# Scan products on whole fp32 operands, a raw weight ring of four, and scan and convolution work dealt out in a fixed order

## The chip, the core and the metric

The kernel runs on one core of one Trainium2 chip. Time is device time in microseconds of one execution, as the median over runs; the kernel before took 1641.52 us (three runs, 1640.8 to 1644.02). The profile is of one further execution of the same program. Engines are named as in the profile: PE (TensorE matmul), PEld (its weight loads), DVE (VectorE), ACT (ScalarE), POOL (GpSimd), SP (the engine whose queue issues most DMAs).

## The reference

One encoder block over 1040 tokens (16 learned meta tokens ahead of 1024 frames) of width 1024, all in float32:

```python
h = h + token_mixer(rmsnorm(h, norm_mix_g), ...)
h = h + channel_mixer(rmsnorm(h, norm_ffn_g), ...)
return rmsnorm(h, norm_final_g)[:, N_META:]
```

The token mixer projects the stream to queries, keys, values and gates of eight heads. Four heads are an mLSTM (queries and keys go through a causal convolution over four tokens and silu; learned input and forget gates with a running maximum), four are a retention with rotary positions and a fixed decay per head. Both are evaluated in chunks, with a state that goes from chunk to chunk:

```python
# mLSTM, one chunk: q, k (C, 128), v (C, 256), state c_st (128, 256), n_st (128)
s = (q @ k.T) * w_intra
num = s @ v + w_inter[:, None] * (q @ c_st)
den = s.sum(-1) + w_inter * (q @ n_st)
h = num / maximum(abs(den), exp(-m_row))[:, None]
c_st = decay * c_st + (w_src[:, None] * k).T @ v
n_st = decay * n_st + (w_src[:, None] * k).sum(0)
# retention: the same without den, with fixed decays in place of the gates
```

Each head's output is normalised per token, multiplied by a gate (sigmoid or silu), and all heads are projected back to width 1024 by w_out. The channel mixer is a gated MLP of width 2816 with a causal convolution over three tokens.

## The kernel before

**Products.** A float32 product is made of three fp32r matmuls: an operand x is split into hi, its rounding to fp32r, by ACT, and lo = x - hi by DVE, and `mm3` and `mm3s` (L487 to L501) sum hi*hi, hi*lo and lo*hi in one PSUM bank. Large projections are cut in the manner of Strassen and Winograd into seven block products (`ROWS`, L545), with sums of the weight blocks made on DVE (`u_fm`, L252) or by accumulating DMAs on POOL's queue (`insum`, L315; `wsum`, L304).

**Stages.** After the first norm and the projection of head 4, the token mixer goes through the heads in the order 4, 0, 1, 2, 3, 5, 6, 7 (`HEADS`; 0 to 3 are mLSTM, 4 to 7 retention), of which (0, 1), (2, 3) and (5, 6) are pairs. For each pair there are a group of query and key steps of the first head (`qk_steps`, 14 steps of 12 matmuls), a group of value steps for both (`v_steps`, 28 steps), the gate steps of the first head (`o_steps`, 14), and the query and key steps and gate steps of the second. Head 7 has a group of its own for values. Then the output product with w_out runs (`mixw`, a `Seven`, L841; its loop at L1475), in steps "1", "65", "73", "4", "2", and the MLP behind it.

**Scan.** A head has nine chunks (16 meta tokens, then eight of 128 tokens; `CH`). `scan_a` (L1052) makes a chunk's scores s = k q and the transposed key, scales and splits them (pt, kw, qd; `split` at L1044). `scan_b` (L1087) splits the values into the ring `vring` (`v_split`, L654), computes the state's update u and the output n by `mm3`, evicts n, forms the new state C and splits it (S). `post_steps` (L1128) normalise a head's chunks, transpose them and multiply by the gate (`sigt`); for all heads but 7 the result goes to DRAM (`mxd`).

**Order.** The tile framework places each engine's instructions by their order in the program and a timeline that it computes; an ordering dependency without a semaphore pins two instructions to each other (`after`, L81). `merge` (L1188) puts the scan steps of one head (`tasks`, L1271; each step is `scan_a` of the next chunk and `scan_b` of this one) between the product steps of the next groups. `gates` (L735), `qk_final` (convolution or rotary, L712) and `tables_make` (L698) each come as one block between groups. Head 7's post steps come behind all product steps (L1416), and the loads for the output product and of the residual behind them (L1419 to L1456).

**Weights.** Units (a weight's load and split) stand in a list and are issued when `need` (L214) asks for one of them, with those whose sizes add up to five places ahead. Raw tiles of 512 KB come from a pool with two slots (`raw_tile`, L181), split tiles from one with three. Among the units are the meta tokens' value products on raw fp32 weights (`meta_raw`, L347: vm), the last two tokens' part of the output product (`last_two`, L288: m; ACT scales a w_out row into two split tiles, which POOL's queue accumulates in DRAM as accd), and the first operands of the output product (`first_right`, L330: r). Loads go through SP's queue in their order.

```python
71    wraw = ctx.enter_context(tc.tile_pool(name="wraw", bufs=2))
225   while i + 1 < len(units) - len(fu) and place[units[i + 1][0]][1] <= j + 5:
226       i += 1
```

Of the kernel before, what the change touches and what calls it, by code (L numbers as in the profile page):

```python
# [60 lines left out]
C_ID, C_M01, C_GV, C_GV0, C_EPS = 0, 128, 256, 260, 264  # L61
C_N = 268
# [3 lines left out]
def body(ctx, tc, h_in, vecs, cst, mask_in, rot, w_v0, w_vp, w_g, w_out, w_up, w_gate, w_down, out):  # L66
# [18 lines left out]
    V, G = nc.vector, nc.gpsimd  # L85
# [29 lines left out]
    def vslot(i, nm, dt=F32):  # L115
        return st.tile([P, 2 * SB if i > 1 else UN], dt, tag=f"v{i}", name=nm)
    w0lo = [vslot(2 + i, f"w0lo{i}", F32R) for i in range(2)]
    sigt = st.tile([P, 2, T - KEEP], F32, name="sig")
    vz = st.tile([P, 2 * DV + 8], F32, name="vz")
# [7 lines left out]
    vring = [tuple(st.tile([P, DV + 2], F32R, name=f"v{x}{i}") for x in "hl") for i in range(2)]  # L127
# [26 lines left out]
    nc.scalar.dma_start(vec, vecs)  # L154
    xload(0)
    nc.vector.memset(epsc, EPS)
    warm = tmp.tile([P, 5], F32, tag="rcol", name="warm")
    nc.scalar.activation(warm[:, 0:1], epsc, AF.Square)
# [5 lines left out]
    for t in vring:  # L164
        G.memset(t[0][:, DV:].bitcast(F32), 0.0)
        G.memset(t[0][:, DV:DV + 1].bitcast(F32), 1.0)
        G.memset(t[1][:, DV:].bitcast(F32), 0.0)
# [12 lines left out]

    def raw_tile(nm):  # L181
        return wraw.tile([P, UN], F32, tag="raw", name="raw_" + nm)

# [11 lines left out]
    def halves(nm, src):  # L195
        r = []
        for i in range(src.shape[1] // HB):
            hi, lo = half_tiles(f"{nm}_{i}")
            x = src[:, i * HB:(i + 1) * HB]
            nc.scalar.copy(hi, x)  # L200
            nc.vector.tensor_tensor(lo, x, hi.bitcast(F32), ALU.subtract)
            r.append((hi, lo))
        return r
# [27 lines left out]
    def loaded(key, srcs):  # L231
        nm = "_".join(str(k) for k in key)
        raw = raw_tile(nm)
        o = 0
        for x in srcs:
            nc.sync.dma_start(raw[:, o:o + x.shape[1]], x)
            o += x.shape[1]
        return raw

    def u_load(key, *srcs):  # L240
        def make():
            raw = loaded(key, srcs)
            return halves("_".join(str(k) for k in key), raw)
        unit(key, 2, make)
# [7 lines left out]
    def u_fm(kind, h, *extra):  # L252
        w = w_g[GI[kind, h]]
        nm = f"{kind}{h}"
        raw = {}

        def form(n):
            if n == 0:
                raw["a"] = loaded((nm, "a"), [w[:, HB:3 * HB]])
                raw["b"] = loaded((nm, "b"), [w[:, 3 * HB:], w[:, :HB]])  # L260
            a0, a1, b0, b1 = (raw[x][:, i * HB:(i + 1) * HB] for x in "ab" for i in (0, 1))
            if n == 2:
                V.tensor_tensor(a0, a0, b0, ALU.add)
                t2, t1 = (half_tiles(f"{nm}_{i}") for i in (2, 3))
                for t, add in ((t1, False), (t2, True)):
                    if add:
                        V.tensor_tensor(a0, a0, b1, ALU.add)
                    nc.scalar.copy(t[0], a0)
                    V.tensor_tensor(t[1], a0, t[0].bitcast(F32), ALU.subtract)
# [6 lines left out]
            return halves(f"{nm}_{n}", {0: a0, 1: a1, 4: b0, 5: b1, 6: a1}[n])[0]  # L276
# [4 lines left out]
        units.extend(extra)  # L281
# [6 lines left out]
    def last_two(k):  # L288
        raw = raw_tile(f"m{k}")
        nc.sync.dma_start(raw, w_out[k])  # L290
        for i, x in enumerate(split_tiles(f"m{k}")):
            x = x.bitcast(F32)
            nc.scalar.activation(x, raw, AF.Copy, scale=mm[:, k, i:i + 1])
            if k == 8:
                nc.sync.dma_start(accd[i], x)
            else:
                G.dma_start(accd[i], x, accum_op=ALU.add)
# [32 lines left out]
    def first_right(k):  # L330
        a = raw_tile(f"fr{k}")
        nc.sync.dma_start(a, mxd[k])
        hi, lo = halves(f"fr{k}", a[:, :HB])[0]
        nc.vector.tensor_tensor(a[:, HB:], a[:, :HB], a[:, HB:], ALU.subtract)
        nc.sync.dma_start(rone[k][:, :HB], hi.bitcast(F32))
        nc.sync.dma_start(rone[k][:, HB:], lo.bitcast(F32))
        nc.sync.dma_start(diff[k], a[:, HB:])
# [3 lines left out]
    def m_units(h):  # L341
        return [(("m", h, b), 2, lambda k=2 * h + b: last_two(k)) for b in range(2)]

    def r_units(*ks):
        return [(("r", k), 1, lambda k=k: first_right(k)) for k in ks]

    def meta_raw(p, s, r):  # L347
        pv = metab.setdefault((p, s), None) or pp(f"pvm{p}_{s}", "tr")
        metab[p, s] = pv
        o = WB[f"{r + 1}{s + 1}"] * UN  # L350
        y = loaded(("vm", p, s, r), [w_vp[p][:, o:o + UN]])
        for k in range(4):
            nc.tensor.matmul(pv[32 * k:32 * k + 32, :DV], ug[:, 4 * r + k, :], y[:, k * DV:(k + 1) * DV],
                             start=r == 0, stop=r == 1, tile_position=(0, 32 * k))
        if r:
            quads(vz[:META, s * DV:(s + 1) * DV], pv, DV)

    metab = {}

    def v_units(p, s):  # L360
        return [(("vm", p, s, r), 0, lambda r=r: meta_raw(p, s, r)) for r in range(2)]
# [6 lines left out]
    for p, (a, b) in enumerate(PAIRS):  # L368
        u_fm("q", a)
# [4 lines left out]
        prev = b  # L374
    u_fm("q", 7, *r_units(2, 3))
    u_fm("v", 7, *r_units(4, 5))
    u_fm("o", 7, *m_units(6), *r_units(6, 7))
# [20 lines left out]
    def wsplit(hi, lo, srcs):  # L398
        o = 0
        for x in srcs:  # L400
            n = x.shape[1]
            nc.scalar.copy(hi[:, o:o + n], x)  # L402
            nc.vector.tensor_tensor(lo[:, o:o + n], x, hi[:, o:o + n].bitcast(F32), ALU.subtract)  # L403
# [3 lines left out]
    def fstep(u, s):  # L407
# [10 lines left out]
        if s == 1:  # L418
            s1 = fpool[0].tile([P, HB], F32, tag="s1", name=f"s1_{u}", bufs=1)
            nc.vector.tensor_tensor(s1, w21, w22, ALU.add)  # L420
            nc.vector.tensor_tensor(w21, w21, w11, ALU.subtract)
            nc.vector.tensor_tensor(w11, s1, w11, ALU.subtract)
            return fsplit(nm, [w11, s1])
        if s == 2:
            nc.vector.tensor_tensor(w12, w12, w11, ALU.subtract)
# [13 lines left out]
    def rms(ss, t0, t1, nm, col, rb, ptags=("tr", "num"), more=()):  # L439
# [5 lines left out]
        for i, (o, w) in enumerate(subs):  # L445
            for a in (ss, *more):
                nc.tensor.matmul(pc[:w, i:i + 1], a[:, o:o + w], cs[:, C_M01 + P - 1:C_M01 + P], start=a is ss, stop=a is (ss, *more)[-1])
        i0 = 1 if subs[0][1] < P else 0
        if i0:
            w = subs[0][1]  # L450
            nc.scalar.activation(col[:w, 0:1], pc[:w, 0:1], AF.Sqrt, bias=epsc[:w], scale=1.0 / D)
            nc.vector.reciprocal(col[:w, 0:1], col[:w, 0:1])
        last["sqrt"] = nc.scalar.activation(col[:, i0:ns], pc[:, i0:ns], AF.Sqrt, bias=epsc, scale=1.0 / D)
        nc.vector.reciprocal(col[:, i0:ns], col[:, i0:ns])
        pr = rps("pr" + nm, ptags[1])
        x = max(0, n - 512)
        for i, (o, w) in enumerate(subs):
            dst = pr[:, o - x:o - x + w] if o >= x else pc[:, 8:8 + w]
            nc.tensor.matmul(dst, col[:w, i:i + 1].to_broadcast([w, P]), ident[:w, :w], start=True, stop=True)
        if x:  # L460
            nc.scalar.copy(rb[:, :x], pc[:, 8:8 + x])
        if rb is not None:
            nc.scalar.copy(rb[:, x:], pr[:, :n - x])
        return pr[:, :n - x]

    def first_norm(r):
# [4 lines left out]
        for x, y in zip(sq, xs):  # L471
            nc.scalar.activation(x, y, AF.Square)
# [4 lines left out]
        for i, x in enumerate(xs):  # L477
# [3 lines left out]
            nc.scalar.copy(h_, x)  # L481
# [5 lines left out]
    def mm3(out, a, b, start, stop):  # L487
        nc.tensor.matmul(out, a[0], b[0], start=start, stop=False, skip_group_check=True)
        nc.tensor.matmul(out, a[0], b[1], start=False, stop=False, skip_group_check=True)
# [1442 lines left out]
```

## Time and profile before

| | before |
|---|---|
| median of three runs | 1641.52 us |
| the profiled execution, its own time | 1638.61 us |
| its span, first to last instruction | 1636.8 us |
| mean granted clock of PE | 0.958 |
| bytes moved by DMA | 256.88 MB |

The span is the time from the first to the last instruction of the profiled execution; its own time has 1.8 us around that. Busy time of PE is modelled from the ends of pipelined matmuls, so it is read together with the count of records and with the granted clock, which is a share of full speed. A line such as "n L489 <- DVE S_7l L1049: 8.3, 4, 3.1" says that instructions of line 489 that write n stood idle until the DVE instruction of line 1049 that writes S_7l had ended: 8.3 us in all, 4 times, at most 3.1 us. Tile names have their pieces' numbers left out in groups of instructions.

### The profile page before, as it was taken

The numbers are of one execution on the slowest core, as the hardware profiler recorded it, in microseconds if no ns is written. First come the engines' busy times: TensorE is split into PE (matmuls) and PEld (weight loads), VectorE is DVE, ScalarE is ACT, GpSimd is POOL, SyncE is SP. The second block draws the span as 40 slices with busy tenths as digits, with TensorE's granted clock in tenths as the row PEclk, the third lists the DMA queues.
The fourth block names the chain that finished last, engine by engine and source line by source line (L and its number), as shares of the span: only waits on it lengthen the run. The fifth ranks groups of instructions, "written<-read, shape, count | busy, mean of one in ns | idle before, by whom it ended". The sixth has DMA issues, their size and how long they took to land.

```text
span 1636.8 us, 26444 instructions
## 1 busy us (share of the span) xinstructions
PE 1516.6 (93%) x9999; PEld 1379.5 (84%) x9999; DVE 1145.1 (70%) x2421; ACT 845.8 (52%) x1764; POOL 131.2 (8%) x190
## 2 busy tenths in 40 slices
PE   5989898898798998988799999999999999999997
PEld 4979798798688997887588899899999999888887
DVE  7586767586566858676586768766666666677757
ACT  5355667584756474636345446544444444444444
POOL 0000021102210020000000000122221000000000
PEclk9989898999899999999799999999999999999999
DMA  5254677748765386649954223788775222953312
GB/s 191 64 119 108 160 179 169 171 142 193 175 159 133 116 186 161 155 143 317 356 165 129 94 88 116 219 218 215 195 185 140 78 78 78 328 187 111 102 52 104
DMA packets 112319, 256.88 MB, mean 157 GB/s; under 512 B 11592, under 2 KB 34832, under 8 KB 111120
## 3 DMA queue, kind: packets, MB, share of 16 engines
q1 hardware_dynamic: 91120, 189.06, 35.1%
q0 software_dynamic: 20928, 66.07, 20.6%
q8 instruction: 78, 1.28, 0.3%
q14 instruction: 49, 0.40, 0.1%
q10 hardware_dynamic: 144, 0.07, 0.0%
HBM read 204.78 MB, written 102.80 MB: 188 GB/s over the span
## 4 chain that ended last, share of the span: by engine, by line
PE 71%; DMA 13%; DVE 7%; issue 5%; ACT 4%; SPq 0%; POOL 0%; DVEq 0%; ACTq 0%; POOLq 0%
PE pdx L498 2%; PE pdx L499 2%; PE pdx L500 2%; PE pup_x L499 2%; PE pup_x L500 2%; PE pup_x L498 2%; PE pga_x L499 2%; PE pga_x L500 2%; PE pga_x L498 2%; PE pdy L499 2%; PE pdy L498 2%; PE pdy L500 2%; DMA accd<-lo_m 2%; DMA raw_vm<-w_vp_d 2%; PE pwx L499 2%
## 5 line engine op out<-in xcount | busy, mean ns | idle before, releaser
L402 ACT CAST hi_up<-raw_up 128x512 fp32r<-128x512 f32 (+1 forms) x52 | 36.4, 719 | 106.8 <-PE pga_z L499 61.2
L498 PE MATMUL pup_x<-uh_g,hi_up 128*128 128x256 f32 (+1 forms) x240 | 67.5, 284 | 1.2 <-ACT uh_g L1332 1.2
L403 DVE TENSOR_TENSOR lo_ga<-fraw_ga,hi_ga 128x512 fp32r<-128x512 f32 (+1 forms) x52 | 41.9, 809 | 37.6 <-ACT hi_ga L402 37.4
L499 PE MATMUL pup_x<-ul_g,hi_up 128*128 128x256 f32 (+1 forms) x240 | 67.5, 283 | 0.1
L500 PE MATMUL pup_x<-uh_g,lo_up 128*128 128x256 f32 (+1 forms) x240 | 66.8, 284 | 0.0
L403 DVE TENSOR_TENSOR lo_up<-raw_up,hi_up 128x512 fp32r<-128x512 f32 (+1 forms) x52 | 41.2, 809 | 35.7 <-ACT hi_up L402 34.9
L402 ACT CAST hi_ga<-fraw_ga 128x512 fp32r<-128x512 f32 (+1 forms) x52 | 36.4, 718 | 47.3 <-PE pup_z L499 22.8
L403 DVE TENSOR_TENSOR lo_d<-rd,hi_d 128x1024 fp32r<-128x1024 f32 (+1 forms) x34 | 37.7, 1113 | 32.9 <-ACT hi_d L402 32.8
L499 PE MATMUL pdx<-ul_d,hi_d 128*128 128x512 f32 (+1 forms) x156 | 58.1, 375 | 0.0
L402 ACT CAST hi_d<-rd 128x1024 fp32r<-128x1024 f32 (+1 forms) x34 | 32.3, 960 | 49.5 <-PE pdy L499 32.6
L500 PE MATMUL pdx<-uh_d,lo_d 128*128 128x512 f32 (+1 forms) x156 | 57.6, 373 | 0.0
L499 PE MATMUL pdy<-ul_d,hi_d 128*128 128x512 f32 x132 | 51.9, 393 | 0.0
L500 PE MATMUL pdy<-uh_d,lo_d 128*128 128x512 f32 x132 | 51.3, 389 | 0.0
L498 PE MATMUL pdx<-uh_d,hi_d 128*128 128x512 f32 (+1 forms) x156 | 48.8, 374 | 0.0
L498 PE MATMUL pdy<-uh_d,hi_d 128*128 128x512 f32 x132 | 48.3, 392 | 0.0
L498 PEld LDWEIGHTS pup_x<-uh_g,hi_up 128*128 128x128 f32 x240 | 45.8, 191 | 2.3 <-ACT uh_g L1332 1.4
L499 PE MATMUL pga_x<-ul_g,hi_ga 128*128 128x512 f32 x120 | 47.6, 397 | 0.0
L500 PE MATMUL pga_x<-uh_g,lo_ga 128*128 128x512 f32 x120 | 47.3, 394 | 0.0
L498 PE MATMUL pga_x<-uh_g,hi_ga 128*128 128x512 f32 x120 | 47.1, 393 | 0.0
L499 PEld LDWEIGHTS pup_x<-ul_g,hi_up 128*128 128x128 f32 x240 | 45.9, 191 | 1.1 <-DVE ul_g L1333 0.3
L500 PEld LDWEIGHTS pup_x<-uh_g,lo_up 128*128 128x128 f32 x240 | 45.0, 190 | 0.8
L309 POOL DMA_DIRECT2D wsd<-w_down_d x33 | 19.0, 680 | 280.5 <-DVE s2up L1581 279.2
(1731 smaller groups left out, 6222.2 us busy)
## 6 DMA issues: line engine op xcount, KB each, us to landing
raw_up<-w_up_d SPq DMA_DIRECT2D x22, 512.0 KB, 4.5
fraw_ga<-w_gate_d SPq DMA_DIRECT2D x22, 512.0 KB, 4.7
acts<-cv SPq DMA_DIRECT2D x44, 256.0 KB, 4.2
wsd<-w_down_d POOLq DMA_DIRECT2D x44, 256.0 KB, 6.6
rd<-wsd SPq DMA_DIRECT2D x22, 512.0 KB, 3.5
wsw<-w_out_d POOLq DMA_DIRECT2D x32, 256.0 KB, 6.1
raw_m<-w_out_d SPq DMA_DIRECT2D x14, 512.0 KB, 4.5
accd<-hi_m POOLq DMA_DIRECT2D x13, 512.0 KB, 7.0
```

What stands on the lines that cost most here:

```text
L309: dep(G.dma_start(x, y), last["pace"], True)
L402: nc.scalar.copy(hi[:, o:o + n], x)
L403: nc.vector.tensor_tensor(lo[:, o:o + n], x, hi[:, o:o + n].bitcast(F32), ALU.subtract)
L498: m.append(nc.tensor.matmul(pt, ah, xh_, start=first and k == 0, stop=False, skip_group_check=True))
L499: nc.tensor.matmul(pt, ah, xl_, start=False, stop=False, skip_group_check=True)
L500: m.append(nc.tensor.matmul(pt, al, xh_, start=False, stop=last and k == n - 1, skip_group_check=True))
```

## The change

- The scan's products take whole fp32 operands: one `matmul` on float32 tiles in place of `mm3`. The splits of pt, kw, qd, v and S, the ring `vring` and the function `split` go. Value tiles become 257 wide per chunk, with a column of ones (set by POOL) that yields den for the mLSTM heads; for retention heads the factor that scaled v scales the key (ACT) and a column of constants `C_GP` scales pt. Head 7's values are transposed in `scan_a` and copied by ACT (`v_turn`).
- Raw weights become a list of jobs that are loaded four ahead of the last one let go (`job`, `jload`, `jget`, `jfree`), in slots that alternate between the old pool of two and a new tag of two. m takes two slots, its source and its second result, and is spread out to one unit per group. r units move one group ahead.
- PE's, DVE's and ACT's instructions are pinned to program order (`watch`) from the end of head 4's gate steps to the seventh step of the output product.
- Scan, convolution, rotary, tables, gates and post work become a list `side` of pieces. `slot` runs one product step and then up to two pieces, with at most one that has PE work, as long as a running estimate of DVE's and ACT's work is not more than 2.5 us ahead of PE's. `drain` runs what is left over at given points.
- `wsum` calls move: one ahead of each group of value steps, one ahead of each group of gate steps. The loads of `wone` move between the fourth and fifth of head 7's gate steps, the first seven steps of the output product run in `slot`, with head 7's scan and post pieces, the residual's loads are issued in the second of them, and those of A1 and B1 ahead of A2 at the end.

The rest of the diff writes `nc.tensor`, `nc.vector` and `nc.scalar` as `PE`, `V` and `AC`.

```diff
+    def watch(ins):
+        nm, kind = ins.engine.name, type(ins).__name__
+        if nm not in RATE or not ins.outs or "DMA" in kind or "Tile" in kind:
+            return
+        if pinned[0] and nm in before:
+            tc.add_manual_dep(ins, before[nm], mybir.DependencyInfo(mybir.DependencyClass.NoSync, mybir.DependencyReason.DATA), reason="order")
+        before[nm] = ins.name
...
     def raw_tile(nm):
+        rawn[0] += 1
+        if jobs and rawn[0] % 2:
+            return st.tile([P, UN], F32, tag="raw2", name="raw_" + nm, bufs=2)
         return wraw.tile([P, UN], F32, tag="raw", name="raw_" + nm)
+    def jload():
+        while len(jraw) < min(len(jobs), jdone[0] + 4):
+            nm, srcs = jobs[len(jraw)]
+            x = raw_tile(nm)
...
+    def jfree(n=1):
+        jdone[0] += n
+        jload()
...
     def u_fm(kind, h, *extra):
+        jb = job(nm + "b", w[:, 3 * HB:], w[:, :HB])
+        ja = job(nm + "a", w[:, HB:3 * HB])
...
-            return halves(f"{nm}_{n}", {0: a0, 1: a1, 4: b0, 5: b1, 6: a1}[n])[0]
+            r = halves(f"{nm}_{n}", {0: a0, 1: a1, 4: b0, 5: b1, 6: a1}[n])[0]
+            if n > 4:
+                jfree()
+            return r
...
     def last_two(k):
+        i = job(f"m{k}", w_out[k])
+        job(f"mt{k}")
+        def make():
+            x, y = jget(i), jget(i + 1)
+            AC.activation(y, x, AF.Copy, scale=mm[:, k, 0:1])
+            AC.activation(x, x, AF.Copy, scale=mm[:, k, 1:2])
+            for t, z in enumerate((y, x)):
...
+                    G.dma_start(accd[t], z, accum_op=ALU.add)
+            jfree(2)
...
-        u_fm("o", a, *v_units(p, 1), *m_units(prev))
-        u_fm("q", b, *(r_units(0, 1) if p == 2 else ()))
-        u_fm("o", b, *(v_units(p + 1, 0) if p < 2 else ()), *m_units(a))
+        u_fm("o", a, *v_units(p, 1), m_unit(prev, 0))
+        u_fm("q", b, *(r_units(0, 1) if p == 2 else ()), m_unit(prev, 1))
+        u_fm("o", b, *(v_units(p + 1, 0) if p < 2 else ()), *(r_units(2, 3) if p == 2 else ()), m_unit(a, 0))
...
+                if (a, b)[f] < H:
+                    G.memset(x[:, :4 * VW].rearrange("p (c j) -> p c j", j=VW)[:, :, DV:], 1.0)
...
         if c < NCH - 1:
             up = pp(f"u{h}_{c}", "upd")
-            mm3(up[:, :nv], kw, v, True, True)
+            PE.matmul(up[:, :nv], kw[:L], v, start=True, stop=True)
         pn = pp(f"n{h}_{c}", "num")
-        scanned[c] = mm3(pn[:L, :nv], pt, v, True, c == 0)
+        scanned[c] = PE.matmul(pn[:L, :nv], pt[:L, :L], v, start=True, stop=c == 0)
         if c:
-            scanned[c] = mm3(pn[:L, :nv], qd, tuple(x[:, :nv] for x in state["S"]), False, True)
+            scanned[c] = PE.matmul(pn[:L, :nv], qd, state["C"][:, :nv], start=False, stop=True)
...
+    def tasks(h):
+        A = [(lambda c=c: scan_a(h, c), 1) for c in range(NCH)]
+        B = [(lambda c=c: scan_b(h, c), 1) for c in range(NCH)]
...
+    def slot(m, lim=2.5, most=2, pe=1):
+        load["slot"] = load["PE"]
+        m()
+        pes = 0
+        for _ in range(most):
+            if not side or side[0][1] and pes == pe or max(load["DVE"], load["Activation"]) - load["PE"] > lim:
+                break
+            pes += one()
...
+    pinned[0] = True
     for p, (a, b) in enumerate(PAIRS):
+        side += rest[0]
+        go(qk_steps(a))
+        side += rest[1]
         steps = v_steps(p)
+        wpace(1)
+        go(steps[:13], 1 if p else 2)
+        drain(f"V{p}")
+        scan, halves_ = tasks(a)
+        side += plain(tables_tasks(a) + qk_tasks(a)) + scan + loads_of(b)
         if p < 2:
             insum(p + 1)
+        go(steps[13:])
         wpace(1)
+        go(o_steps(a))
+        drain(f"qkT{a}", 3)
...
+    go(steps[4:])
     issue(len(units) - len(fu))
+    mixw.pump()
+    jobs.clear()
...
+    for t in range(KW - 1):
+        for u in (t, t + 1):
+            mixw.prep(u)
+        for js in ((0, 1), (2, 3)):
+            slot(lambda: mixw.mms(t, js=js), pe=2)
...
+    drain("end")
+    pinned[0] = False
```

More of the change, by code (lines that the diff above doesn't have):

```diff
@@ L1266, in body @@
     usplit("S1", "S1", "uh3", "ul3")
-    tables_load(4)
-    gates()
-    qk_final(4)
-    def tasks(h):
-        return [lambda: scan_a(h, 0)] + [ab(h, c) for c in range(NCH)] + [f for p in range(3) for f in post_steps(h, p)]
-    side = tasks(4)
-    def take(n):
-        r = side[:n]
-        del side[:n]
-        return r
     wjobs = list(range(8))
-    def group(steps, n, start=0, stop=None):
-        merge(steps, take(n), start, stop)
     def wpace(n):
@@ L1288, in wpace, with plain, loads_of @@
             wsum("w", wjobs.pop(0))
-    insum(0)
-    group(o_steps(4), 5, 5)
+    def plain(fs):
+        return [(f, 0) for f in fs]
+    def loads_of(h):
+        return [(lambda: tables_load(h), 0)]
+    tables_load(4)
+    gate_gen = gates()
+    gate_tasks = [(lambda: next(gate_gen, None), 1)] * 6
+    insum(0)
+    scan, halves_ = tasks(4)
+    rt = plain(qk_tasks(4))
+    first = rt + scan[:12]
+    side += [x for y in zip(gate_tasks, first) for x in y] + first[len(gate_tasks):]
+    rest = scan[12:] + loads_of(0), halves_
```

727 lines of the change are left out of this document (379 added, 348 removed).

## The prediction

> **What bounds the kernel now.** I read the page's head first, then the busy times by stretch.
>
> ```profile
> span 1636.8 us, 26444 instructions
> PE 1516.6 (93%) x9999; PEld 1379.5 (84%) x9999; DVE 1145.1 (70%) x2421; ACT 845.8 (52%) x1764; POOL 131.2 (8%) x190
> ```
>
> PE is busy for 93% of the span, so time is gained only where PE waits or runs below its full clock. The next rows say where that is. Columns: stretch, its length, busy us (and records) of PE, PEld, DVE, ACT and POOL, granted clock, DMA share, GB/s.
>
> ```profile
> 85.00:806.00 721.00, 633.12 (x4801) 597.71 (x4800) 498.57 (x1336) 429.26 (x1017) 71.44 (x95) 0.92 0.66 172
> 806.00:1637.00 831.00, 820.48 (x4750) 722.64 (x4748) 586.96 (x967) 376.21 (x684) 55.43 (x79) 0.99 0.49 146
> 85.00:150.00 65.00, 55.28 (x411) 51.24 (x410) 44.61 (x105) 31.43 (x68) 0.82 (x1) 0.89 0.51 123
> 150.00:760.00 610.00, 548.84 (x4267) 524.83 (x4266) 427.31 (x1158) 377.82 (x901) 69.77 (x93) 0.94 0.64 163
> 760.00:806.00 46.00, 29.00 (x129) 21.64 (x128) 26.66 (x73) 20.02 (x48) 0.85 (x1) 0.74 1.01 367
> 510.00:600.00 90.00, 90.00 (x756) 87.79 (x755) 70.71 (x203) 51.03 (x140) 6.63 (x9) 1.00 0.48 129
> ```
>
> From 806 us on (the gated MLP, which the change leaves alone) PE idles 10.5 of 831 us at clock 0.99: nothing is to be had there. From 85 to 806 us, the token mixer that the change rewrites, PE idles 88 of 721 us and has clock 0.92 besides. The stretch from 510 to 600 us, with product steps and scan mixed as elsewhere, shows what this mixture costs undisturbed: 756 records in 90 us, 8.40 per us. By that rate the 411 records of 85 to 150 us need 48.9 us, so 16 are lost; the 4267 of 150 to 760 us need 508, so 102 are lost. In 760 to 806 us many records are 512 wide, so I take idle plus clock there: 17 + 0.26 x 29.0 = 24.5. **Lost now: 142.5 us; the undisturbed stage: 721 - 142.5 = 578.5 us.**
>
> Next the chain that ended last, in order of time (start, us, what), at two of the places where PE falls behind.
>
> ```profile
> 282.34 6.15 DMA raw_vm<-w_vp_d
> ...
> 289.32 4.89 DMA raw_m<-w_out_d
> ...
> 306.35 8.53 DMA accd<-lo_m
> ...
> 428.73 15.00 DMA raw_q_b<-w_g_d
> ```
>
> The path runs through one DMA after another: with two raw slots a weight, a meta weight, and the two accumulations of a w_out row follow each other in series, and the next group's weight stands behind. What PE itself waits for in the stage, and what SP's queue waits for:
>
> ```profile
> PE n L489 <- DVE S_7l L1049: 8.3, 4, 3.1
> PE pvm L353 <- DMA raw_vm<-w_vp_d: 7.6, 4, 2.8
> PE n L488 <- ACT den L1113: 6.5, 4, 5.8
> ...
> SPq L236 <- DVE lo_o L201: 88.5, 5, 62.1
> ```
>
> (total us, times, longest us.) The largest PE waits are scan products standing for splits (S_7l) and for ACT; the queue that loads weights stood 88.5 us for DVE to let go of a raw tile. The stage is bound by PE, with losses from late weights and from splits queued on DVE and ACT.
>
> **The change part by part.**
>
> *Whole fp32 operands in the scan.* Every chunk has up to three products: u, n from pt, n from the state; 8 heads x (8 + 9 + 8) = 200. Each was three fp32r matmuls and becomes one fp32 matmul, which the trace records as two passes. Prices, from PE's order of starts (start us, us, line, operation):
>
> ```profile
> 573.82 0.28 PE L498 MATMUL pv2x<-hi_vp,u22h 128*128 128x256 f32 x1
> ...
> 575.47 0.28 PE L488 MATMUL u<-vh,kwh 128*128 128x256 f32 x1
> ...
> 576.79 0.38 PE L1057 MATMUL s<-qT,kT 128*128 128x128 f32 x2
> 577.01 0.27 PE L1062 MATMUL s<-cs,kT 128*128 128x128 f32 x1
> L353 PE MATMUL pvm<-raw_vm,ug x96: 376/403/636, 92.7 to 590.4; 128*32 128x256 f32 x96
> ```
>
> Between the first two starts lie 14 matmuls of 256 columns: 1.65 / 14 = 0.118 us each, 0.354 for three. The fp32 product s has 128 columns and takes 0.22 us for its two passes, 0.86 ns per column and pass. No fp32 product of 256 columns over the whole array is in the trace. Estimate by columns: 2 x 0.22 = 0.44. Lower end, a pass no dearer than that of 128 columns: 0.22. Upper end, the meta products' passes one after the other, median 0.403 each: 0.81. I take 0.44, since s is the same operation on the same array, while the meta products run four side by side and 0.403 is a latency. **Cost: 200 x (0.44 - 0.354) = 17, say 18 us on PE**; ends -27 and +91.
>
> The splits go. Sums of the lines of pt, qd and S (ACT copies, then DVE subtractions), and the groups of v and kw:
>
> ```profile
> sum 721.00, ACT 63.53; mean ACT 63.53
> sum 721.00, DVE 62.35; mean DVE 62.35
> L670 DVE TENSOR_TENSOR vl<-v,vh 128x256 fp32r<-128x256 f32 x32 | 13.4, 418 | 7.1 <-ACT vh L669 7.0
> L675 DVE SCALAR_TENSOR_TENSOR vl<-v,cs,vh 128x256 fp32r<-128x256 f32 x24 | 11.3, 472 | 2.4 <-ACT vh L674 2.4
> L1071 DVE SCALAR_TENSOR_TENSOR kwl<-s,cols,kwh 128x128 fp32r<-128x128 f32 x32 | 11.0, 344 | 0.2
> L1081 DVE TENSOR_TENSOR kwl<-s,kwh 128x128 fp32r<-128x128 f32 x32 | 9.0, 282 | 2.2 <-ACT kwh L1080 2.1
> ```
>
> DVE loses 62.4 + 13.4 + 11.3 + 11.0 + 9.0 = 107 of 499 us, ACT at least 63.5 of 429. That is not a gain by itself, since PE is the bound; it shortens the way from s to n and takes scan waits out of the 102 us.
>
> *Four raw slots, loads issued as a slot comes free.* vm, m and weight no longer follow each other as in the chain at 282 us, and m writes into raw slots, so its accumulations stop holding the ring of splits. What stays late is the next group's first weight. A group's b tile is let go with its form 5 and its a tile with form 6; the look-ahead of `need` (five places) issues these at product steps 2 and 4 and the next group's first cut at step 6, two steps after its load is asked for. A step is 12 x 0.118 = 1.42 us and one scan piece (25 products of 0.44 us and 17 to 20 small ones in 18 pieces, about 0.65 us): 4.1 us of cover. The landings (KB, median us):
>
> ```profile
> raw_q_a<-w_g_d SPq DMA_DIRECT2D x7, 512.0 KB, 6.9
> raw_o_a<-w_g_d SPq DMA_DIRECT2D x7, 512.0 KB, 7.3
> ```
>
> So ACT stands some 3 us at the cut. **The new order is fixed on PE, DVE and ACT**, so behind that cut stand the lo subtraction, the step's own eviction and the next scan piece's kw and pt, and PE stops at that scan piece. Sixteen groups are of this kind; without the first and the last, which are in the ends below, 14 x 3 = **42 us of loss stay** (0 to 14 x 10.9, the latter by the 15.00 us landing).
>
> *Dealing out.* Convolution, rotary, tables, gates and post work come one piece per product step, instead of in blocks that fill DVE. Their instruction counts stay. At the start (16 us lost) the gates' chain goes between the o steps of head 4, I take half: 8 us stay. At the end (24.5 lost) head 7's rest goes beside the first seven steps of the output product. DMA has share 1.01 there, and the same loads remain; wone moves up by ten product steps, but A2 now stands behind B1, whose last tile waits for the last wone. I take 10 us (0 to 24.5).
>
> The v tiles get their column of ones by memsets on POOL, behind the weight sums:
>
> ```profile
> 360.20 1.10 POOL L318 DMA_DIRECT2D vs<-w_vp_d  x2 [52.99 <-DVE qd L1074]
> ...
> 386.35 0.81 POOL L302 DMA_DIRECT2D vs<-vs  x1 [7.82 <-DMA vs<-vs]
> ```
>
> POOL is held about 26 us; the memset in question is twelve product steps (25 us) after that sum is issued, and its reader later still. I cost it at nothing, covered by these steps; if it were 10 us late, 20 us for the two pairs that have it.
>
> **Sum.** 578.5 + 18 + 42 + 8 + 10 = 656.5 us for the stage, 64.5 less than 721. The profiled execution took 1638.6 us (span 1636.8): 1574.1. It was 2.9 below the median 1641.5: **1577 us**, 4% less.
>
> A clock row belongs to that sum, since it holds no loss of clock:
>
> ```profile
> 100.00:110.00 10.00, 9.70 (x60) 8.63 (x60) 7.61 (x17) 2.31 (x6) 0.00 (x0) 0.69 0.39 147
> ```
>
> PE is busy for 9.70 us here, but makes 60 records instead of 84: clock 0.69 after the waits before it, 24 / 8.40 = 2.9 us. [...]
>
> **The rivals.**
> 1. *No late cuts.* The loads land within the cover (raw_m took 4.89 us above), and only the ends stay: 578.5 + 18 + 18 = 614.5, 106.5 less: 1535 us. For it: 90 us without any loss around 510 us. Against: the medians 6.9 and 7.3.
> [...]
> 3. *Slower: the fixed order turns each late weight into a standstill.* Place: first cut of a group, on ACT. If landings are like the 15.00 us of raw_q_b, 10.9 us are lost in each of 14 groups, 153 instead of 42: +111, 1688 us. It decides from (142.5 - 18 - 18) / 14 = 7.6 us per group, a landing of 11.7 us. For it: before, an instruction that could run was free to be placed ahead; the DMA share will rise, as the same bytes move in less time (0.66 x 721 / 656.5 = 0.72). Against: medians near 7.
> 4. *The fp32 passes are dearer*, 0.81 per product: +91 instead of +18, 1650 us. Against: s at 0.22.
> 5. *Not what it says:* DVE and ACT get free, but PE waits for something else of equal length, and the time stays.
>
> **How the numbers follow.** Forecast 0.50, rival 1: 0.13, rival 2: 0.17, rival 3: 0.14, rival 4: 0.04, rival 5: 0.02. Faster by more than 0.2% (what a measurement of this kernel can tell from no change) are the forecast and rivals 1 and 2: 0.80; same 0.02 and a bit of the edges, 0.03; slower 0.17. The range takes in the forecast, rival 2, most of rival 1 and the smaller forms of rival 3: 1530 to 1640 us; outside stay about 0.2. The forecast's own range is 1550 to 1605.
>
> **What would show it.** In the changed profile: 400 fp32 passes in place of 600 matmuls, about 0.22 us from start to start; DVE near 390 us and ACT near 360 in the stage; clock at 0.97 or more between 150 us and the end of the mixer; no pvm wait for DMA; the remaining PE waits at the first scan piece after step 6 of a group, with ACT waiting for a raw load. The stage's end, where the steps "65" begin, should come near 740 us instead of 806. The prediction is wrong if PE waits of over 7 us return at most group starts, if the passes take 0.4 us, or if the 831 us behind the mixer change.

## The result and the profile after

The change makes the kernel slower. The median is 1704.11 us over four runs (1701.65 to 1709.01), against 1642.43 us for the kernel before in the same comparison (1640.8 to 1644.02): a ratio of 1.0379, 95% interval 1.0353 to 1.0405. The forecast was 1577 us. The head of the page of the profile after, and the shares of the chain of work that ended last, by engine, first before and then after:

```profile
span 1699.9 us, 25284 instructions
PE 1536.6 (90%) x9799; PEld 1391.6 (82%) x9799; DVE 1083.3 (64%) x2089; ACT 767.7 (45%) x1489; POOL 132.0 (8%) x192
...
PE 71%; DMA 13%; DVE 7%; issue 5%; ACT 4%; SPq 0%; POOL 0%; DVEq 0%; ACTq 0%; POOLq 0%
...
PE 66%; DVE 15%; ACT 12%; DMA 5%; issue 2%; SPq 0%; DVEq 0%; ACTq 0%
```

DMA falls from 13% of that chain to 5%; DVE and ACT together rise from 11% to 27% of it, though both are less busy than before (DVE 1145.1, ACT 845.8 us). The path goes less through late weights, as the change means it to, and more through two engines that are busy for 64% and 45% of the span. The busy times by stretch, columns as in the prediction:

```profile
85.00:869.00 784.00, 661.45 (x4630) 618.20 (x4629) 436.43 (x1004) 354.77 (x747) 73.00 (x103) 0.91 0.60 159
869.00:1699.90 830.90, 810.78 (x4709) 713.71 (x4707) 587.29 (x971) 373.37 (x681) 55.66 (x79) 0.99 0.49 144
500.00:520.00 20.00, 10.29 (x80) 9.18 (x78) 10.71 (x23) 11.27 (x20) 3.75 (x5) 0.74 0.84 168
```

The second row, 830.9 us against 831.0, is the part behind the mixer: untouched. All of the loss is in the first, which has grown from 721 to 784 us. In the prediction's own terms: undisturbed it would take 578.5 + 18 = 596.5 us, so 187.5 are lost where the forecast had 60. PE idles 784 - 661.45 = 122.6 us of it (88 before), and the other 65 are PE busy beyond its undisturbed time. Of these 52 go to the clock, added up over PE's busy records (40 before); the stage's mean of 0.91 would give 60, but it counts idle time too. The 13 that are left say that the undisturbed time was itself put that much too low. The third row is a short stretch in which half of the time is gone. What PE waits for between 80 and 880 us (total us, times, longest us):

```profile
PE tr L1223 <- DVE mx L1230: 41.6, 12, 6.2
PE s L1130 <- DVE pt L1145: 30.5, 8, 9.7
PE s L1130 <- DVE pt L1150: 14.2, 7, 5.5
PE pwx L563 <- ACT hi_w L467: 3.7, 1, 3.7
```

Two kinds make up 86 of the 122.6 us: the transposes of `post_steps` stand until DVE has multiplied the ones before by the gate (mx), and a chunk's scores s stand until DVE has read the scores before (pt). Neither is a product step of a projection. What DVE itself waited for there:

```profile
DVE pt L1150 <- ACT kw L1142: 32.1, 20, 7.6
DVE mx L1230 <- DMA mxd<-mx: 29.4, 11, 7.4
DVE pt L1145 <- ACT kw L1142: 28.0, 22, 2.7
```

pt does not use kw; the two read the same PSUM tile s, and kw comes first in the program. The timeline of the largest standstill shows what kw stands behind (start us, us, what; in brackets the idle time before it and what ended it):

```profile
504.47 2.33 DVE L787 SCALAR_TENSOR_TENSOR qT<-rawq,vec,qT 128x512 f32<-128x512 f32 x3 [2.69 <-ACT qT L783]
...
504.97 0.29 PE L1130 MATMUL s<-qT,kT 128*128 128x16 f32 x2
...
506.53 0.28 PE L565 MATMUL po3x<-uS2h,lo_o 128*128 128x256 f32 x1
...
507.65 2.32 DVE L787 SCALAR_TENSOR_TENSOR kT<-rawk,vec,kT 128x512 f32<-128x512 f32 x3
509.88 0.41 DVE L642 TENSOR_TENSOR sig<-sig,po3y 128x256 f32<-128x256 f32 x1
510.22 0.68 DVE L319 TENSOR_TENSOR raw_o3a<-raw_o3a 128x512 f32<-128x512 f32 x1
...
510.99 0.62 ACT L249 CAST hi_o<-raw_o3a 128x512 fp32r<-128x512 f32 x1 [5.15 <-DVE raw_o3a L319]
...
512.37 1.15 ACT L343 ACTIVATE raw_mt<-raw_m,mm 128x1024 f32<-128x1024 f32 x1 [0.50 <-DVE lo_o L250]
513.54 1.15 ACT L344 ACTIVATE raw_m<-raw_m,mm 128x1024 f32<-128x1024 f32 x1
...
514.60 0.37 ACT L640 ACTIVATE sig<-po3x 128x258 f32<-128x258 f32 x1
514.87 0.62 ACT L792 ACTIVATE qT<-qT 128x512 f32<-128x512 f32 x1
...
515.38 0.62 ACT L792 ACTIVATE kT<-kT 128x512 f32<-128x512 f32 x1
515.90 0.36 ACT L1142 ACTIVATE kw<-s,cols 128x128 f32<-128x128 f32 x1
...
516.29 0.17 DVE L1145 TENSOR_TENSOR pt<-s,A 128x16 f32<-128x16 f32 x1 [2.60 <-ACT kw L1142]
516.52 0.80 PE L1130 MATMUL s<-qT,kT 128*128 128x128 f32 x2 [9.71 <-DVE pt L1145]
```

PE makes the scores at 504.97. ACT, whose next instruction is a weight's cut, stands 5.15 us for DVE, which has a convolution of q and of k ahead of that weight's block sum. Then ACT has the meta weight's two scalings and the silus of q and k to do, and only then kw, 10.9 us after s was there. DVE stands in turn, and PE, whose next instruction by the fixed order is the next chunk's s, stands 9.71 us, with product steps behind it. Each engine idles, one after the other. No weight is late here.

### The profile page after: what moved, and what is told of

It reads as the page before. It is cut to its first block, busy times and chain, and to the rows that moved or that the text cites. A ratio compares the mean times of both kernels' runs of the same rounds, so it can differ in the third digit from the quotient of the medians.

```text
span 1699.9 us, 25284 instructions
## 1 busy us (share of the span) xinstructions
PE 1536.6 (90%) x9799; PEld 1391.6 (82%) x9799; DVE 1083.3 (64%) x2089; ACT 767.7 (45%) x1489; POOL 132.0 (8%) x192
## 4 chain that ended last, share of the span: by engine, by line
PE 66%; DVE 15%; ACT 12%; DMA 5%; issue 2%; SPq 0%; DVEq 0%; ACTq 0%
PE pdx L563 2%; PE pdx L564 2%; DMA mxd<-mx 2%; PE pdx L565 2%; PE pup_x L564 2%; PE pup_x L565 2%; PE pga_x L564 2%; PE pup_x L563 2%; PE pga_x L565 2%; PE pga_x L563 2%; PE pdy L564 2%; PE pdy L563 2%; PE pdy L565 2%; PE pwx L563 1%; PE pwx L565 1%
## 5 line engine op out<-in xcount | busy, mean ns | idle before, releaser
L467 ACT CAST hi_up<-raw_up 128x512 fp32r<-128x512 f32 (+1 forms) x52 | 36.4, 718 | 106.0 <-PE pga_z L564 61.2
L1130 PE MATMUL s<-qT,kT 128*128 128x128 f32 (+1 forms) x144 | 30.2, 292 | 44.7 <-DVE pt L1145 30.5
L1130 PEld LDWEIGHTS s<-qT,kT 128*128 128x128 f32 x144 | 23.4, 200 | 47.9 <-DVE pt L1145 32.1
L1230 DVE SCALAR_TENSOR_TENSOR mx<-tr,vec,sig 128x386 f32<-128x386 f32 (+2 forms) x42 | 24.0, 572 | 49.8 <-DMA mxd<-mx 29.4
L467 ACT CAST hi_d<-rd 128x1024 fp32r<-128x1024 f32 (+1 forms) x34 | 32.3, 960 | 49.4 <-PE pdy L564 32.6
```

The costliest lines, as they stand in the source:

```text
L467: AC.copy(hi[:, o:o + n], x)
L1130: PE.matmul(s[:, :L], k, q, start=True, stop=True)
L1230: return V.scalar_tensor_tensor(dst, tr[:, x0 - t0:x1 - t0], vec[:, g:g + 1], sig(b, p)[:, x0 - a0:x1 - a0], ALU.mult, ALU.mult)
```

## The experiments

Two theories were set against each other at first. **A:** the order that `watch` fixes on PE, DVE and ACT makes each engine wait at the place where its turn stands. **B:** the mx ring of two is held by slow stores, which share SP's queue with the weight loads that now run four ahead. Edits are against the kernel after, unless another is named. Gains and losses between two runs are differences of their ratios times 1642 us, since each ratio is taken to runs of the kernel before made beside it.

### The order let go: `free_order`

```diff
-    pinned[0] = True
```

> The changed kernel without the pinned order; everything else stays. Theory A, the fixed order: PE's waits of s for pt (30.5 + 14.2 = 44.7 us in the changed kernel) come from ACT and DVE working their queues in program order; free to be placed ahead, kw and pt come early, and about 45 us go: near 1660 us. Theory B, SP's queue: the result's stores mxd<-mx stand behind raw loads, which does not depend on the pinned order: the waits of tr for mx (41.6 us) stay, and the time stays within 15 us of 1704.

Measured: 1590.2 us, ratio 0.9699 [0.9656, 0.9742]; 0.068 x 1642 = 112 us faster than the kernel after, and 3% faster than the one before. Its busy times by stretch, and what PE waits for from 80 to 880 us:

```profile
85.00:763.00 678.00, 628.64 (x4605) 588.42 (x4604) 421.40 (x998) 365.18 (x753) 72.47 (x103) 0.96 0.68 181
763.00:1594.00 831.00, 813.31 (x4717) 715.52 (x4715) 586.94 (x970) 373.97 (x680) 55.61 (x79) 0.99 0.49 146
```

```profile
PE s L1130 <- DVE pt L1150: 7.0, 2, 4.4
PE n L1175 <- ACT den L1189: 5.8, 1, 5.8
...
PE tr L1223 <- DVE mx L1230: 4.1, 5, 1.8
```

The mixer takes 678 us: 81.5 are lost, of which PE idles 49.4. So the pins cost the mixer 106 us, 73 of them as idle time of PE and most of the rest by the clock (0.91 with the pins, 0.96 without). Both kinds of wait have gone from 86 us to 11. At the place of the timeline above the same instructions stand in another order:

```profile
444.24 0.77 DVE L787 SCALAR_TENSOR_TENSOR kT<-rawk,vec,kT 128x526 f32<-128x526 f32 x1
...
444.91 0.69 DVE L250 TENSOR_TENSOR lo_o<-raw_o3b,hi_o 128x512 fp32r<-128x512 f32 x1
...
446.11 0.62 ACT L249 CAST hi_o<-raw_o3a 128x512 fp32r<-128x512 f32 x1 [1.46 <-PE po3y L564]
...
449.60 0.29 PE L1130 MATMUL s<-qT,kT 128*128 128x16 f32 x2
...
453.25 0.35 ACT L1142 ACTIVATE kw<-s,cols 128x128 f32<-128x128 f32 x1
```

DVE puts the weight's work between single steps of the convolution, ACT cuts raw_o3a before s is there, and kw comes 3.7 us after s instead of 10.9. PE's order differs as well: the next s (454.76) has some 35 product matmuls ahead of it since the first one, where the fixed order had 12. Theory A holds, and it is the whole of the loss: without the pins the change is a gain. Its size was not foreseen, though: 45 us were expected back and 112 came. Without the pins, too, the order of each engine is settled when the program is built, only by the framework's timeline and not by hand. The runs compare these two orders; whether another order by hand would do as well was not tried.

### The stores and the ring of mx: `mx_store_on_act`, `three_mx`, `free_three_mx`

```diff
-            nc.sync.dma_start(mxd[i][:, a0 - MA:e - MA], mx[:, :e - a0])
+            AC.dma_start(mxd[i][:, a0 - MA:e - MA], mx[:, :e - a0])
```

> The changed kernel with the store of a head's result (mxd<-mx) issued from ACT's queue and not from SP's, where it stands behind raw loads that wait for their slots. Theory B: DVE's wait for mxd<-mx (29.4 us) and most of PE's wait of tr for mx (41.6 us) go, 30 to 45 us with the clock: 1660 to 1675 us. Theory A: those waits move to another place in the same fixed queues, and under 10 us are won.

Measured: 1705.28 us, ratio 1.0392 [1.0349, 1.0435], as theory A expects. The wait stays:

```profile
PE tr L1223 <- DVE mx L1230: 42.4, 11, 6.2
```

For the other two, the ring has three tiles, in the kernel after and in that without the pins:

```diff
-            mx = mxp.tile([P, WMAX], F32, tag="mx", name=f"mx{h}_{p}_{b}", bufs=2)
+            mx = mxp.tile([P, WMAX], F32, tag="mx", name=f"mx{h}_{p}_{b}", bufs=3)
```

> The changed kernel (all three orders pinned) with three mx tiles in place of two. Issuing the store from ACT's queue changed nothing, so the theory is now the store's own time: two tiles, each held until its store has landed (6 to 9 us beside the weight sums), with six halves of a head dealt out one per product step. Then PE's wait of tr for mx (41.6 us) falls by a third to a half, and the time by 10 to 25 us: 1680 to 1695. If tr waits for DVE's place in its queue, it stays within 5 us of 1704.

> The changed kernel without any pinned order, with three mx tiles. Without the order it took 1590 us, with PE's wait of tr for mx at 4.1 us and DVE's for the store at 15.6. The third tile takes part of these: 1582 to 1590, the fastest version. A gain of none would say that those waits lie beside others.

Measured: 1694.77 us, ratio 1.0296 [1.0235, 1.0356], 14 us less than the kernel after and within the 10 to 25 expected, though the two intervals just touch. The reason given for it was wrong: DVE's wait for the store halves (14.8 us from 29.4), but PE's wait goes to 38.4 us only, and PE idles as long in the mixer as before the edit. Without the pins 1590.2 us, ratio 0.9679 [0.9655, 0.9704], the same as `free_order` and not the gain that was hoped for. Theory B falls: neither the queue nor the size of the ring sets PE's wait, and with the pins a third tile is worth 14 us at most.

### Whole fp32 operands alone: `fp32_alone`

The kernel before, with the scan's `mm3` replaced and the splits taken out, in its own order and with its own ring of weights:

```diff
-        scanned[c] = mm3(pn[:L, :nv], pt, v, True, c == 0)
+        scanned[c] = nc.tensor.matmul(pn[:L, :nv], pt[:L, :L], v, start=True, stop=c == 0)
```

> The kernel before with whole fp32 operands in the scan and nothing else of the change (values are copied, not split, into a ring with a column of ones; two raw slots, free order, the old places). If the fp32 products cost what the starts of s say, PE gets 18 us more work, of which waits for splits (n for S 8.3, n for pt 3.6, u for vh 3.8 us) give back up to 15: 1640 to 1660 us. If the fp32 operands are what made the changed kernel slow, it comes near 1700.

Measured: 1623.4 us, ratio 0.9882 [0.9827, 0.9936], 19 us faster than before and 17 below the range expected. What PE waits for from 80 to 806 us adds up to 75 us against 87 before; from 85 to 806 us DVE is busy for 426 us against 499 and ACT for 387 against 429. So the dearer products are more than paid for, and the shorter way through ACT and DVE is the likely reason. The edit also gives the tile qd a second buffer; its part was not measured alone.

### kw and pt the other way round: `pt_before_kw`

```diff
-            AC.activation(kw, s[:, P:2 * P], AF.Copy, scale=w)
...
         pre[c] = (pt, kw, qd)
```

with the removed line put behind pt, ahead of `pre[c]`.

> The changed kernel with pt (DVE) ahead of kw (ACT) in scan_a, as the kernel before had them. In the changed kernel DVE waits 60 us for kw before pt, both reading one PSUM bank, and PE waits 44.7 us for pt before the next s. If that order is the cause of the wait, s for pt shrinks to below 15 us and some 25 us go: near 1680 us. If the bank is late because ACT's queue is late (kw must be read out as well before the next s), the wait is only renamed to kw, and the time stays within 8 us.

Measured: 1703.23 us, ratio 1.0383 [1.0341, 1.0425]. PE's wait has only changed its name:

```profile
PE s L1130 <- ACT kw L1151: 44.0, 14, 9.5
```

44.0 us, as the two rows of s had together (44.7). ACT now waits for pt in 47 places (61 us) where DVE waited for kw in 42 (60 us). Which of the two readers goes first is not the cost. At the place of the timeline pt is now done at 509.9 us, and kw still comes only at 511.95, behind the same scalings and silus in ACT's queue; in other places it is DVE that comes late.

### A second PSUM bank for s: `two_s_banks`

```diff
-        s = pp(f"s{h}_{c}", "sA")
+        s = pp(f"s{h}_{c}", ("sA", "tr")[c % 2])
```

> The changed kernel (pinned) with the scores s in two PSUM banks in turn (sA, and tr, which the halves use too). If PE's 44.7 us of s for pt come from the one bank, so that a late kw or pt stops PE at the very next s, the wait falls below 20 us and the time to 1670 to 1690. If kw and pt are later than two scan pieces, or the shared bank tr takes the wait over, it stays above 1695.

Measured: 1723.19 us, ratio 1.0468 [1.0405, 1.0531]: 15 us slower than the kernel after. The wait for pt goes, but the bank is shared with other users of the tag, and their readers take its place:

```profile
PE s L1130 <- DVE vz L576: 27.8, 5, 7.0
```

The kernel's eight PSUM buffers (`PSB`) each have a use already, and none was taken out to give s a bank of its own; whether that would help was not tried.

### One engine pinned alone: `pin_pe_only`, `pin_act_only`, `pin_dve_only`

```diff
-        if pinned[0] and nm in before:
+        if pinned[0] and nm in before and nm in ("PE",):
```

and the same with "Activation" and with "DVE".

> The changed kernel with only PE's instructions pinned to program order; DVE and ACT are placed freely. The changed kernel took 1704 us, without any pinned order 1590: 114 us to divide. Theory A1, PE's own order: PE stops at a scan piece whose kw or pt is late although the next product step is ready, so pinning PE alone costs most of it: 1660 to 1700 us. Theory A2, the two feeding queues: kw and pt are late only because ACT and DVE work in program order, waiting for each other; with these free PE's order costs little: 1590 to 1620 us.

> The changed kernel with only ACT's instructions pinned to program order. Theory A2 with ACT as the late queue (DVE waits 60 us for kw, and PE for pt behind that): 1640 us or more. Theory A1: ACT's order alone costs under 30 us, below 1620.

> The changed kernel with only DVE's instructions pinned to program order. Theory A2 with both queues at fault: DVE alone costs a third to a half, 1630 to 1650 us. Theory A1: below 1620. If each engine's order alone costs little and all three together 114 us, the cost lies in their waiting for each other in turn.

Measured: PE 1655.08 us, ratio 1.0083 [1.006, 1.0107]; ACT 1642.16, 1.0014 [0.9992, 1.0037]; DVE 1661.49, 1.0124 [1.0049, 1.0199]. Against `free_order` these are losses of 63, 52 and 70 us. Each engine alone costs about half of what all three cost together, and they do not add up (185 against 112). So neither theory holds in its pure form: PE alone stays just under the 1660 to 1700 us of A1 and above the 1590 to 1620 of A2; ACT alone fits A2, and DVE alone costs more than A2 gave it. With PE alone pinned the wait of the transposes is whole and that of s is nearly gone:

```profile
PE tr L1223 <- DVE mx L1230: 41.2, 20, 6.1
...
PE s L1130 <- DVE pt L1150: 4.9, 3, 2.1
```

With ACT alone pinned the transposes wait 6.1 us and s for pt 0.2 us, with DVE alone 13.6 and 1.6 us. So the transposes stand because PE's place for them is fixed, whereas s stands only when PE's order and that of at least one of the other two are fixed together; which of these it takes was not tried. What ACT's and DVE's order cost when fixed alone is spread over many short waits of PE, none over 14 us in all, and was not followed up.

### Which instructions must not be held: `cuts_unpinned`, `pieces_unpinned`, `plain_unpinned`, `scan_unpinned`, `halves_unpinned`

A flag leaves one kind of work out of the pinned order and keeps the pins among all the rest:

```diff
-        if pinned[0] and nm in before:
-            tc.add_manual_dep(...)
-        before[nm] = ins.name
+        if not loose[0]:
+            if pinned[0] and nm in before:
+                tc.add_manual_dep(...)
+            before[nm] = ins.name
```

It is set around a weight unit's cut and sum (cuts), around every dealt-out piece (pieces), around those without PE work (plain), around `scan_a` and `scan_b` (scan), or around the transposing halves of the post steps (halves).

> The changed kernel with the weight units (cuts into hi and lo, sums of weight blocks, m, vm, r) left out of the pinned order; product steps and dealt-out pieces stay pinned. Theory C: the cuts, each a chain of ACT and DVE instructions in turn, stand in the fixed queues ahead of evictions and of the scan's kw and pt; free, they get out of the way and half or more of the 114 us comes back: 1600 to 1650. Theory D: the dealt-out pieces themselves (conv, rotary, post, scan) hold each other; the cuts give back under a quarter: above 1675.

> The changed kernel with the dealt-out pieces (scan, conv, rotary, tables, gates, post) left out of the pinned order; product steps and weight units stay pinned. Theory D: 1600 to 1650. Theory C: above 1675. If both this and the run before come to 1600 to 1650, the loss is in the mixture of the two in one order, not in either.

> The changed kernel with only the pieces without PE work (conv, rotary, tables, post statistics) left out of the pinned order. All pieces free took 1621 us of 1704, 83 us less. If the scan's kw and pt are late because conv and tables stand ahead of them on ACT and DVE, this brings 40 us or more: below 1665, and s for pt falls from 44.7 us to below 15. If they are late by their own place in the order, it brings under 15: above 1690.

> The changed kernel with only scan_a and scan_b left out of the pinned order. If the loss is that PE must run a scan piece at its place, though a product step is ready behind it, and that kw and pt keep their place behind conv, this brings 40 us or more: below 1665, with s for pt below 10 us. If the wait only moves to another pinned piece, under 15: above 1690.

> The changed kernel with only the post halves (transposes, mx, store) left out of the pinned order. PE's wait of tr for mx is 41.6 us in the changed kernel, and a third mx tile took 9 us off the time. If PE's and DVE's fixed place of a half costs that wait, 30 to 50 us go: 1655 to 1675, tr for mx below 12 us. If the stores and the one tr bank set it whatever the order, under 15 us go.

| left out of the order | median us | ratio, interval | against the kernel after |
|---|---|---|---|
| cuts | 1694.47 | 1.0294 [1.0233, 1.0354] | -14 us |
| plain pieces | 1716.38 | 1.0456 [1.0433, 1.0479] | +13 us |
| scan | 1653.64 | 1.0074 [1.0049, 1.0099] | -50 us |
| halves | 1668.75 | 1.0166 [1.0119, 1.0212] | -35 us |
| all pieces | 1621.26 | 0.9849 [0.9777, 0.9921] | -87 us |

Scan and halves each let go add up to 85 us, all pieces let go give 87, of 112. These are two executions each, with intervals of 4 to 12 us to either side, and the plain pieces alone go the other way, so the near equality is partly luck; that most of the loss lies in scan and halves is not. What PE waits for tells the two apart. First with the scan free, then with the halves free:

```profile
PE tr L1230 <- DVE mx L1237: 50.6, 9, 7.9
```

```profile
PE s L1132 <- DVE pt L1147: 23.1, 5, 10.1
PE s L1132 <- DVE pt L1152: 14.0, 5, 5.8
PE tr L1230 <- DVE mx L1237: 10.2, 8, 2.3
```

With the scan free its own wait is all but gone (0.3 us) and the transposes' stays (50.6 us); with the halves free the transposes' falls to 10.2 and that of s stays (37.1). Each wait goes with the pieces that it is named after. The cuts, on which the prediction put its loss, are worth 14 us at most; the intervals of that kernel and of the kernel after just touch. The plain pieces, convolution and tables, give nothing back when they alone are let go, which neither branch of the expectation foresaw: the wait of s falls by 19 us (16.2 + 9.2 are left), and that of the transposes grows by 13 (to 54.7). So the convolution that holds up kw in the timeline is part of the queue and not a cause that can be taken out alone.

### The ring of four without the pins: `free_two_ahead`

```diff
-        while len(jraw) < min(len(jobs), jdone[0] + 4):
+        while len(jraw) < min(len(jobs), jdone[0] + 2):
...
-    pinned[0] = True
```

> The changed kernel without the pinned order and with raw weights loaded two ahead in place of four (the slots stay). If the loads four ahead bring a good part of what the free order wins over the kernel before (1642 to 1590), this is 15 us or more above 1590. If it is fp32 operands and the dealing out alone, it stays within 8 us of 1590.

Measured: 1636.85 us, ratio 0.9976 [0.995, 1.0001]. Against `free_order` 45 us are lost, and ACT stands for the meta weight, which needs two slots at once:

```profile
ACT raw_mt L343 <- DMA raw_m<-w_out_d: 65.7, 11, 15.2
```

Loading four ahead is worth these 45 us in this kernel, where a meta weight that takes two slots leaves room for no other load when only two are allowed. Without it and without the pins the new kernel is slower than `fp32_alone` (0.9976 against 0.9882), so dealing the work out in pieces, with the meta weight's two slots that come with it, brings nothing on top of the fp32 operands until loads go four ahead.

## Why the prediction was wrong

**The step that failed** is the term "Sixteen groups are of this kind; without the first and the last, which are in the ends below, 14 x 3 = 42 us of loss stay". It charged the fixed order only where a weight comes late, on ACT, and took dealing out as free but for the ends. The loss in the stage was 187.5 us in place of 60 (42 + 8 + 10). The wait that this term prices did not come: in the profile after no cut on ACT and no block sum on DVE waits for a load, and the only wait of ACT for a DMA from 80 to 880 us is

```profile
ACT raw_mt L343 <- DMA diff<-raw_fr: 17.6, 3, 7.4
```

The runs show instead that the order costs 112 us (`free_order`), some 85 of them through scan pieces and transposes that are held at their place on PE, DVE and ACT (`scan_unpinned`, `halves_unpinned`, `pieces_unpinned`), and 14 at most through cuts. The sentence "behind that cut stand the lo subtraction, the step's own eviction and the next scan piece's kw and pt, and PE stops at that scan piece" named the right victim, and the timeline at 504.97 us shows exactly that queue; but what keeps ACT there is a convolution on DVE, not a load. A chain over three engines in fixed order was costed as a wait on one.

**The rival that came nearest**, the third (1688 us, slower), had its side right, and nearly its size, by luck and for the wrong reason. It asked for 10.9 us at each first cut; PE's waits for cuts are not among the large ones, and freeing the cuts takes back 14 us, not 111. Its argument "before, an instruction that could run was free to be placed ahead" is what the runs bore out, for the scan rather than for the weights. The transposes' wait stood in no rival, though in the profile before it was already the largest of PE's rows from 80 to 880 us:

```profile
PE tr L1157 <- DVE mx L1164: 10.5, 4, 6.1
```

**The clock.** One scan piece per step did not keep PE's gaps short. A piece needs PE, ACT, DVE and PE again; when one of these is late, the next piece is held too, and gaps of up to 9.7 us came. The forecast's sum holds no loss of clock, and its clock of 0.97 or more was 0.91 in the stage. Behind the gap of 9.71 us the granted clock is 0.52 from 516.5 to 520 us and 1.00 in the next 4 us; before, the clock of 0.69 from 100 to 110 us comes behind a wait of 2.79 us. PE has 10 gaps over 4 us in the stage, against 4 before, where the clock is 0.92. Without the pins the rows of PE's waits from 80 to 880 us hold three of over 4 us (5.8, 5.7 and 4.4), and the stage's clock is 0.96. No run here changed the length of a gap alone.

**The price of the fp32 product was right.** Starts in PE's order after (granted clock 1.00 from 323.0 to 324.6 us):

```profile
323.21 0.60 PE L1173 MATMUL u<-v,kw 128*128 128x257 f32 x2
323.65 0.60 PE L1175 MATMUL n<-v,pt 128*128 128x257 f32 x2
324.08 0.60 PE L1177 MATMUL n<-C,qd 128*128 128x257 f32 x2
```

0.43 to 0.44 us from start to start, where 0.44 was taken by columns from s; the fourth rival's 0.81 falls. That the relief of ACT and DVE "is not a gain by itself" was too careful: `fp32_alone` gained 19 us net of the dearer products, with qd's second buffer.

**DVE and ACT.** ACT is busy 354.8 us in the stage (forecast near 360), DVE 436.4 (near 390). The 107 us that were taken off DVE are a sum of single durations, and neighbours on DVE overlap in the records (above, qT's three steps of 504.47 us, at 2.33 us, end at 506.80; the next instruction starts at 506.71). The busy time counts an overlap once. The single durations in the stage add up to 583 us before and 471 after, so they fell by 112, near the 107; but the records overlapped by 85 us before and by 34 after, and the busy time fell by 62 only.

**The loads.** No wait for a DMA is left among PE's rows from 80 to 880 us, DMA's share of the chain fell to 5%, and loading four ahead is worth 45 us where the order lets it work. With the pins gone, the stage loses 81.5 us where 60 were forecast, and the time is 1590 us against 1577. The number is near, but not for the reason given: there, too, cuts and block sums of q and o weights wait 3.0 us for loads in all (2.2 on ACT, 0.8 on DVE), not 42.

**The time between 869 us and the end** stayed at 831, as said.

## What to carry to other kernels

A fixed order over several engines is costed by the cross-engine chain of each piece (here PE, ACT, DVE, PE), with all that stands ahead of each link on its own engine, and not by the busy sums, which fell here while the time rose. Let the order be free first and measure the other parts without it: the fp32 operands (19 us) and the ring of four (45 us) were gains that the pins (112 us) hid. Where a wait is named after one of two readers of a tile, swapping them shows whether their order matters; here only the name of the wait changed.

## What the runs showed of the hardware

Two engines that read one PSUM tile did so one after the other, although they read different columns: in the profile after none of the 64 kw overlaps a pt in time. There DVE's pt stood 60.1 us for ACT's kw (32.1 + 28.0), and with the program turned round (`pt_before_kw`) ACT's kw stood 61.2 us for pt (31.9 + 29.3), with PE's wait unchanged (44.7 and 44.0 us). In the traces these waits end with a semaphore event of the other engine, so the program orders them; whether the chip needs that order, these runs don't tell.

An fp32 product of 257 columns is two passes at 0.43 to 0.44 us together in the profile after (323.21 to 324.08 us), 0.85 ns per column and pass, as for 128 columns in the profile before (0.22 us, 0.86 ns): at these two widths the price per column is the same.
